# Gelu-branch and first merge projections in turn, attention five steps later, and recurrence weights with hi and lo stacked in the contraction

## The chip, the cores and the metric

The kernel runs on one core of one Trainium2 chip. Its engines are TensorE (PE in the profile, PEld for its weight loads), VectorE (DVE), ScalarE (ACT), GpSimd (POOL) and SyncE (SP), which issues the DMAs. The metric is the device time in microseconds of one execution; the number shown is the median of the runs.

## What is computed

A decoder trunk of two layers on 256 tokens of 1024 features, all in float32: a half-step SwiGLU, a hybrid mixing block, another half-step SwiGLU, and a gated per-layer embedding, each with RMSNorm in front. The change lies in the mixing block alone:

```python
proj = h @ w_in[i]
rx, rgate, q, k, v, f_logit, ga, gb = jnp.split(proj, split_idx, axis=-1)
rx = causal_dwconv(rx, conv_w[i], conv_b[i])
ya = rg_lru(rx, rg_wa[i], rg_ba[i], rg_wx[i], rg_bx[i], rg_lambda[i])
ya = (ya * jax.nn.gelu(rgate)) @ w_rnn_out[i]
yb = forgetting_attention(q, k, v, f_logit, f_b[i], q_norm[i], k_norm[i]) @ w_attn_out[i]
merged = jax.nn.sigmoid(ga + mb_a) * ya + jax.nn.sigmoid(gb + mb_b) * yb
x = x + merged @ w_o[i]
```

`rg_lru` multiplies each of 16 blocks of 64 channels by its own two 64 x 64 matrices (`rg_wa` for the gate r, `rg_wx` for the gate i), takes sigmoids, forms a decay and an input from them, and runs a linear recurrence along the tokens. Attention has 8 heads of 128.

## The kernel before

Activations lie transposed, features on the 128 partitions (8 tiles of 128 features) and 256 tokens along the free dimension. A product in float32 is made from halves: each operand is split into `hi`, its value rounded to the matmul's format, and `lo`, the rest, and hi·hi + hi·lo + lo·hi is accumulated in PSUM (`mm3`, lines 304 to 306 for weights as the stationary operand, 309 to 311 for activations; `mm2`, lines 344 to 347, does two of the three with one matmul of 512 columns).

Weights stream from HBM. The list `plan` gives their order; class `Weights` loads a chunk of about 1 MB into one of three raw buffers `wr` (line 84, on SP's queue), and splits each half of it, a *unit* of eight 128 x 128 tiles, into `wh` on ACT (line 95) and `wl` on DVE (line 96). Five units fit; `W.next()` hands out one and emits the split of the one four units ahead.

The mixing block of a layer goes through these steps in program order:

- Eight `rx` projections. `rx_post` applies the norm, runs the convolution (`conv`) and splits its output `xc` into `xch` (ACT, line 522) and `xcl` (DVE, line 523).
- The `v` projection and a first part of q and k. Between their parts `gates(m)` does the block products of tile m: for each of the two gates a 128 x 128 weight tile with the two 64 x 64 blocks on its diagonal, zeros elsewhere, and `mm3`, so six matmuls of 256 columns. ACT takes the tanh of each gate (`thr`, `thi`, lines 554 and 555), then come two deferred steps, `s1` (clamp of `thr` on DVE; exp, tanh and square on ACT) and `s2` (`tq` on DVE at line 565, and `xc` times the gate i at line 566). `root` takes a square root of all `tq`.
- The remaining q and k projections, with the recurrence (`scan`, lines 575 and 576) between their parts.
- 24 *fillers*, one unit each: 8 for the gelu branch (`f < KT`), which have four more DVE operations and three more ACT operations than the rest, 8 for merge gate A and 8 for merge gate B, which have one DVE and one ACT operation.
- Attention, in four steps for each head (`step_a` transposes, `step_b` scores and softmax, `step_c` transposes, `step_d` the weighted sum into `ot`). They are hung on the parts of the second q and k group and on the fillers through `slots`: head h begins at slot 4 + (5h+1)//2, where slots 0 to 7 are the parts and 8 to 31 the fillers.
- The merge: `ya` (recurrence branch) and `yb` (attention) products by pairs of output tiles, their gated sum `mg`, and the product with `w_o`.

Small steps are handed to a queue (`defer`) and taken from it by `tick` and `drain`. The order in this text is not the order on the engines: the framework's planner (`schedule_with_timeline_sim=True`) orders each engine's instructions by a simulated timeline, with the order of the text as priority, and only marked instructions keep their place.

Of the kernel before, what the change touches and what calls it, by code (L numbers as in the profile page):

```python
# [10 lines left out]
F32 = mybir.dt.float32  # L11
F32R = mybir.dt.float32r
# [4 lines left out]
P = 128  # L17
# [26 lines left out]
HC = S + 4 * P + 1  # L44
WARM = 9
MF, MA, MB, MO = 6, 8, 2, 6


class Weights:
# [70 lines left out]
def trunk(ctx: ExitStack, tc: tile.TileContext, head, xT, pT, vec, w1i, w1o, wf, wqk, wv, wg, wro, wao, wo, w2i, w2o,  # L120
# [16 lines left out]
    def big(shape, dt, s):  # L137
        return bp.tile(shape, dt, name=nm(s), tag="big")
# [21 lines left out]
    for l in range(DEPTH):  # L160
        plan += [(w1i[l, j], [1024, 1024]) for j in range(2 if l == 0 else 0, FT)]
        plan += [(w1o[l, m, :, h * 1408:(h + 1) * 1408], [768, 640]) for m in range(KT) for h in range(2)]
        plan += [(wf[l, 0, c], [1024, 1024]) for c in range(4)]
        plan += [(wv[l, c], [4 * VC, 4 * VC]) for c in range(4)]
        plan += [(wqk[l, qk, cb, hf], [1024, 1024]) for cb in range(2) for qk in range(2) for hf in range(2)]
        plan += [(wf[l, f, c], [1024, 1024]) for f in (1, 2, 3) for c in range(4)]
        plan += [(wrao, [1024, 1024]) for c in range(4) for wrao in (wro[l, c], wao[l, c])]
        plan += [(wo[l, c], [1024, 1024]) for c in range(4)]
        plan += [(w2i[l, j], [1024, 1024]) for j in range(FT)]
        plan += [(w2o[l, m, :, h * 1408:(h + 1) * 1408], [768, 640]) for m in range(KT) for h in range(2)]  # L170
        plan += [(wpg[l, c], [1024, 1024]) for c in range(4)]
# [331 lines left out]
    def mix(l, n, wgp):  # L503
        a = n.act
        R2 = small(TT)
        xc = big([P, KT, S], F32, "xc")
        xch = big([P, KT, S], F32R, "xch")
        xcl = big([P, KT, S], F32R, "xcl")


        def rx_post(m, ps):
            t = rxp[m % NRX]
            V.tensor_tensor(out=t[:, 3:], in0=ps[:, 0:S], in1=n.RB, op=ALU.mult)
            A.activation(out=xc[:, m], in_=t[:, 0:S], func=AF.Identity, scale=col(l, "convw", m), bias=col(l, "convb", m))

            def conv():
                for k in range(1, 4):
                    V.scalar_tensor_tensor(out=xc[:, m], in0=t[:, k:k + S], scalar=col(l, "convw", 8 * k + m),
                                           in1=xc[:, m], op0=ALU.mult, op1=ALU.add)

            def split():
                A.activation(out=xch[:, m], in_=xc[:, m], func=AF.Copy)
                V.tensor_tensor(out=xcl[:, m], in0=xc[:, m], in1=xch[:, m].bitcast(F32), op=ALU.subtract)
            defer(conv, split)

        two = (mmbank, atbank)
# [20 lines left out]

        def gates(m):
            ps = two[m % 2]("g")
            for g in range(2):  # L550
                c = slice((m * 2 + g) * P, (m * 2 + g + 1) * P)
                mm3(ps[:, g * S:(g + 1) * S], wg_hi[:, c], wg_lo[:, c], xch[:, m], xcl[:, m], True, True)
            thr, thi, th, a2 = work(s="thr"), work(s="thi"), work(s="th"), work(s="a2")
            A.activation(out=thr, in_=ps[:, 0:S], func=AF.Tanh, scale=0.5, bias=hcol(l, "ba", m))
            A.activation(out=thi, in_=ps[:, S:], func=AF.Tanh, scale=0.5, bias=hcol(l, "bx", m))
            sc, nsc = sp[:, l, 0, m:m + 1], sp[:, l, 1, m:m + 1]

            def s1():
                V.tensor_scalar(out=thr, in0=thr, scalar1=-1.0, scalar2=None, op0=ALU.max)
                A.activation(out=at[:, m], in_=thr, func=AF.Exp, scale=nsc, bias=nsc)  # L560
                A.activation(out=th, in_=thr, func=AF.Tanh, scale=sc, bias=sc)
                A.activation(out=a2, in_=at[:, m], func=AF.Square)

            def s2():
                V.scalar_tensor_tensor(out=tq[:, m], in0=a2, scalar=1.0, in1=th, op0=ALU.add, op1=ALU.mult)
                V.scalar_tensor_tensor(out=xc[:, m], in0=thi, scalar=1.0, in1=xc[:, m], op0=ALU.add, op1=ALU.mult)
            defer(s1, s2)
# [177 lines left out]
        slots = [[] for _ in range(4 * KT)]  # L745
        for h in range(NH):
            for i, f in enumerate((step_a, step_b, step_c, step_d)):
                slots[4 + (5 * h + 1) // 2 + i].append((f, h))

        def attend(i):  # L750
            for f, h in reversed(slots[i]):
# [34 lines left out]
        qk_group(1, 0, during1(0))  # L786
        qk_group(1, 1, during1(1))
        drain()
        for f in range(3 * KT):
            filler(f)  # L790
            attend(KT + f)
            tick()
        drain()

# [156 lines left out]
def _layout(inputs):  # L951
# [20 lines left out]
                   axis=1)  # L972
    vf = np.concatenate([v, f], axis=2)
    wv = vf.reshape(L, KT, P, 4, VC).transpose(0, 3, 2, 1, 4).reshape(L, 4, P, KT * VC)
    wg = np.zeros((L, P, KT, 2, P), np.float32)
    for i, t in enumerate((g["rg_wa"], g["rg_wx"])):
        t = t.reshape(L, KT, 2, 64, 64)
        for b in range(2):
            wg[:, b * 64:(b + 1) * 64, :, i, b * 64:(b + 1) * 64] = t[:, :, b].transpose(0, 2, 1, 3)
    wg = wg.reshape(L, P, KT * 2 * P)  # L980
    wpe = g["ple_w_proj"].reshape(L, 2, P, KT, P).transpose(0, 2, 3, 1, 4).reshape(L, P, KT * 2 * P)

# [15 lines left out]
    vec[:, :, VEC["fb"]:VEC["fb"] + NH] = g["f_b"][None]  # L998
    put("mba", g["merge_b"][:, :D])
    put("mbb", g["merge_b"][:, D:])  # L1000
    put("ba", g["rg_ba"])
    put("bx", g["rg_bx"])
    put("pb", g["ple_b_gate"])

    w1i = ffn_in(g["ffn1_w_in"])
# [29 lines left out]
```

## Time and profile before

| | |
|---|---|
| median of three runs | 1323.04 us (1323.02 to 1323.09) |
| profiled execution | 1323.63 us, span 1321.8 us |
| PE busy | 1311.8 us (99%), 8610 matmuls |
| DVE busy | 1076.1 us (81%) |
| ACT busy | 815.5 us (62%) |
| DMA | 240.21 MB, mean 182 GB/s |

The span runs from the first to the last instruction; the profiled execution's own time is 1.8 us more. Busy times of one engine count overlapping instructions once; PE's matmuls overlap, so that the duration of one is more than its share of the engine's time.

### The profile page before, as it was taken

How to read it: one execution, taken by the hardware profiler on the slowest of the kernel's cores; microseconds unless marked ns; L12 is line 12 of the kernel's file. 1: busy time of each engine (PE TensorE's matmuls, PEld its weight loads, DVE VectorE, ACT ScalarE, POOL GpSimd, SP SyncE). 2: the span in 40 equal slices, each digit the busy share in tenths (PEclk: the TensorE clock that was granted, in tenths of full speed). 3: DMA queues.
4: the chain of work that ended last, by engine and by line, in shares of the span. 5: the costliest groups of instructions: out<-in, count | busy, mean ns of one | idle time of the engine just before them, and what ended most of it. 6: DMA issues, size and time to landing. Idle time of an engine off the chain costs nothing.

```text
span 1321.8 us, 22442 instructions
## 1 busy us (share of the span) xinstructions
PE 1311.8 (99%) x8610; PEld 1197.7 (91%) x8610; DVE 1076.1 (81%) x2142; ACT 815.5 (62%) x1470; POOL 34.1 (3%) x43
## 2 busy tenths in 40 slices
PE   9999999999999999999999999999999999999997
PEld 8888899889999888889988888998999998888897
DVE  7998769899757899876789877698997678988756
ACT  6665656868655666565566555578677556655653
POOL 1000000020000000000000000000200000000000
PEclk9999999999999999999999999999999999999998
DMA  8654665445435555456545546644543455554650
GB/s 292 243 179 160 212 225 193 158 164 175 151 128 191 196 189 189 162 184 231 187 165 192 188 153 212 241 161 159 193 166 128 161 190 191 192 191 142 213 187 33
DMA packets 37259, 240.21 MB, mean 182 GB/s; under 512 B 4128, under 2 KB 4768, under 8 KB 14368
## 3 DMA queue, kind: packets, MB, share of 16 engines
q1 hardware_dynamic: 36720, 238.25, 51.3%
q8 instruction: 68, 1.11, 0.3%
q10 hardware_dynamic: 432, 0.52, 0.1%
q14 instruction: 39, 0.32, 0.1%
HBM read 237.71 MB, written 1.05 MB: 181 GB/s over the span
## 4 chain that ended last, share of the span: by engine, by line
PE 99%; DMA 0%; DVE 0%; ACT 0%; SPq 0%; POOLq 0%; issue 0%; DVEq 0%
PE mm L347 20%; PE mm L345 11%; PE at L347 11%; PE at L345 6%; PE f L304 3%; PE f L305 3%; PE f L306 3%; PE qk L309 2%; PE qk L311 2%; PE qk L310 2%; PE mm L306 2%; PE mm L304 2%; PE mm L305 2%; PE ya L347 2%; PE mm L344 2%; PE at L344 2%
## 5 line engine op out<-in xcount | busy, mean ns | idle before, releaser
L95 ACT ACTIVATE wh<-wr 128x1024 fp32r<-128x1024 f32 (+2 forms) x476 | 467.4, 986 | 308.0 <-PE mm L347 90.8
L96 DVE TENSOR_TENSOR wl<-wr,wh 128x1024 fp32r<-128x1024 f32 (+2 forms) x476 | 537.7, 1132 | 142.3 <-ACT wh L95 136.9
L347 PE MATMUL mm<-h,wh 128*128 128x512 f32 x616 | 219.2, 394 | 0.0
L347 PE MATMUL at<-h,wh 128*128 128x512 f32 x616 | 218.4, 394 | 0.0
L345 PE MATMUL mm<-h,wl 128*128 128x256 f32 x704 | 182.4, 281 | 0.0
L345 PE MATMUL at<-h,wl 128*128 128x256 f32 x704 | 181.7, 281 | 0.3 <-DVE wl L96 0.2
L347 PE MATMUL mm<-f,wh 128*128 128x512 f32 x504 | 176.8, 394 | 0.0
L345 PE MATMUL mm<-f,wl 128*128 128x256 f32 x528 | 144.0, 280 | 0.0
L345 PEld LDWEIGHTS at<-h,wl 128*128 128x128 f32 x704 | 131.8, 188 | 8.8 <-DVE wl L96 0.8
L345 PEld LDWEIGHTS mm<-h,wl 128*128 128x128 f32 x704 | 131.8, 188 | 7.8 <-DVE wl L96 0.4
L347 PEld LDWEIGHTS mm<-h,wh 128*128 128x128 f32 x616 | 115.6, 188 | 22.5
L347 PEld LDWEIGHTS at<-h,wh 128*128 128x128 f32 x616 | 114.9, 188 | 21.9
L347 PEld LDWEIGHTS mm<-f,wh 128*128 128x128 f32 x504 | 94.4, 188 | 20.8
L304 PE MATMUL f<-h,wh 128*128 128x256 f32 x384 | 108.6, 283 | 0.0
L306 PE MATMUL f<-h,wl 128*128 128x256 f32 x384 | 108.4, 282 | 0.0
L305 PE MATMUL f<-h,wh 128*128 128x256 f32 x384 | 108.4, 282 | 0.0
L345 PEld LDWEIGHTS mm<-f,wl 128*128 128x128 f32 x528 | 99.4, 188 | 2.1
L305 PEld LDWEIGHTS f<-h,wh 128*128 128x128 f32 x384 | 72.3, 188 | 0.1
L304 PEld LDWEIGHTS f<-h,wh 128*128 128x128 f32 x384 | 72.3, 188 | 0.1
L306 PEld LDWEIGHTS f<-h,wl 128*128 128x128 f32 x384 | 72.4, 189 | 0.0
L381 ACT ACTIVATE sum<-mm 128x256 f32<-128x256 f32 x112 | 40.2, 376 | 49.3 <-PE mm L347 49.3
L382 DVE TENSOR_TENSOR sum<-mm,sum 128x256 f32<-128x256 f32 x112 | 44.9, 417 | 15.0 <-ACT sum L381 15.0
(291 smaller groups left out, 2857.6 us busy)
## 6 DMA issues: line engine op xcount, KB each, us to landing
wr<-in_w2i SPq DMA_DIRECT2D x44, 1024.0 KB, 4.8
wr<-in_w1i SPq DMA_DIRECT2D x41, 1024.0 KB, 4.8
wr<-in_wf SPq DMA_DIRECT2D x32, 1024.0 KB, 4.8
wr<-in_w1o SPq DMA_DIRECT2D x32, 704.0 KB, 4.0
wr<-in_w2o SPq DMA_DIRECT2D x32, 704.0 KB, 4.0
wr<-in_wqk SPq DMA_DIRECT2D x16, 1024.0 KB, 4.8
wr<-in_wv SPq DMA_DIRECT2D x8, 1032.0 KB, 4.9
wr<-in_wro SPq DMA_DIRECT2D x8, 1024.0 KB, 4.8
```

The lines of the kernel that those rows point to most:

```text
L95: self.nc.scalar.activation(out=hi[:, c], in_=src[:, c], func=AF.Copy)
L96: self.nc.vector.tensor_tensor(out=lo[:, c], in0=src[:, c], in1=hi[:, c].bitcast(F32), op=ALU.subtract)
L304: T.matmul(ps, lhsT=wh, rhs=xh, start=first, stop=False)
L305: T.matmul(ps, lhsT=wh, rhs=xl, start=False, stop=False)
L306: T.matmul(ps, lhsT=wl, rhs=xh, start=False, stop=last)
L309: T.matmul(ps, lhsT=xh, rhs=wh, start=first, stop=False)
L310: T.matmul(ps, lhsT=xh, rhs=wl, start=False, stop=False)
L344: T.matmul(ps, lhsT=wh, rhs=t, start=True, stop=False, skip_group_check=True)
L345: T.matmul(ps[:, 0:S], lhsT=wl, rhs=t[:, 0:S], start=False, stop=False, skip_group_check=True)
L347: T.matmul(ps, lhsT=wh, rhs=t, start=False, stop=last, skip_group_check=True)
L381: A.activation(out=o, in_=ps[:, S:], func=AF.Copy)
L382: V.tensor_tensor(out=o, in0=ps[:, 0:S], in1=o, op=ALU.add)
```

## The change

Three edits, all in the mixing block.

1. *Stacked weights.* For each tile of 128 channels, which holds two blocks b of 64, the rows of the new 128 x 128 weight tile b hold block b's matrix twice, once in the lower and once in the upper 64 rows, and its columns hold both gates, r and i (in the other order for b = 1). The moving operand `xs[b]` stacks hi and lo of block b's 64 channels on the partitions. One matmul with the hi weights and one with the lo weights then give both gates of the block, with one product more than `mm3` has (lo·lo). Four matmuls of 256 columns take the place of six. The split writes `xs` by halves of the partitions, two ACT and two DVE instructions in place of one and one; half of them write to the other half of the partitions than they read. ACT's two tanh now give r and i of one block each (`t2`, a tile of 512 columns from the pool with three buffers), a DMA on SP's queue moves the half that holds i to the partitions of its channels in `thi` (two DMAs of 64 partitions x 1 KB per tile), and the clamp writes `thr` by two instructions of 64 partitions. The biases are put in the same order on the host.
2. *Order of the fillers.* Instead of 8 gelu, 8 gate A, 8 gate B: two gelu and two gate A in turn, four times, then 8 gate B. The chunks of `wf` are loaded in the same order.
3. *Attention five slots later.* Head h begins at slot 9 + (5h+1)//2 (`AT0`).

```diff
+AT0 = 9
 ...
-        plan += [(wf[l, f, c], [1024, 1024]) for f in (1, 2, 3) for c in range(4)]
+        plan += [(wf[l, f, c], [1024, 1024]) for c in range(4) for f in (1, 2)]
+        plan += [(wf[l, 3, c], [1024, 1024]) for c in range(4)]
 ...
-        xch = big([P, KT, S], F32R, "xch")
-        xcl = big([P, KT, S], F32R, "xcl")
+        xs = [big([P, KT, S], F32R, "xs") for _ in range(2)]
+        lower, upper = slice(0, 64), slice(64, P)
 ...
             def split():
-                A.activation(out=xch[:, m], in_=xc[:, m], func=AF.Copy)
-                V.tensor_tensor(out=xcl[:, m], in0=xc[:, m], in1=xch[:, m].bitcast(F32), op=ALU.subtract)
+                for b, own, other in ((0, lower, upper), (1, upper, lower)):
+                    A.activation(out=xs[b][own, m], in_=xc[own, m], func=AF.Copy)
+                    V.tensor_tensor(out=xs[b][other, m], in0=xc[own, m], in1=xs[b][own, m].bitcast(F32),
+                                    op=ALU.subtract)
 ...
         def gates(m):
             ps = two[m % 2]("g")
-            for g in range(2):
-                c = slice((m * 2 + g) * P, (m * 2 + g + 1) * P)
-                mm3(ps[:, g * S:(g + 1) * S], wg_hi[:, c], wg_lo[:, c], xch[:, m], xcl[:, m], True, True)
+            for b in range(2):
+                c = slice((m * 2 + b) * P, (m * 2 + b + 1) * P)
+                T.matmul(ps[:, b * S:(b + 1) * S], lhsT=wg_hi[:, c], rhs=xs[b][:, m], start=True, stop=False)
+                T.matmul(ps[:, b * S:(b + 1) * S], lhsT=wg_lo[:, c], rhs=xs[b][:, m], start=False, stop=True)
             thr, thi, th, a2 = work(s="thr"), work(s="thi"), work(s="th"), work(s="a2")
-            A.activation(out=thr, in_=ps[:, 0:S], func=AF.Tanh, scale=0.5, bias=hcol(l, "ba", m))
-            A.activation(out=thi, in_=ps[:, S:], func=AF.Tanh, scale=0.5, bias=hcol(l, "bx", m))
+            t2 = work2(s="tg")
+            for b, own, other in ((0, lower, upper), (1, upper, lower)):
+                c = slice(b * S, (b + 1) * S)
+                A.activation(out=t2[:, c], in_=ps[:, c], func=AF.Tanh, scale=0.5, bias=hcol(l, ("ba", "bx")[b], m))
+                nc.sync.dma_start(out=thi[own], in_=t2[other, c])
 ...
             def s1():
-                V.tensor_scalar(out=thr, in0=thr, scalar1=-1.0, scalar2=None, op0=ALU.max)
+                for b, own in ((0, lower), (1, upper)):
+                    V.tensor_scalar(out=thr[own], in0=t2[own, b * S:(b + 1) * S], scalar1=-1.0, scalar2=None,
+                                    op0=ALU.max)
 ...
-                slots[4 + (5 * h + 1) // 2 + i].append((f, h))
+                slots[AT0 + (5 * h + 1) // 2 + i].append((f, h))
 ...
-        for f in range(3 * KT):
+        turns = [f + m for m in range(0, KT, 2) for f in (0, 1, KT, KT + 1)] + list(range(2 * KT, 3 * KT))
+        for i, f in enumerate(turns):
             filler(f)
-            attend(KT + f)
+            attend(KT + i)
             tick()
```

On the host, `_layout` builds the new weight tiles and puts the two biases in the order of the gates' halves.

## Rows read from the trace of the kernel before

**Rows 1.** The page's head: the span, the busy time of each engine (share of the span, number of instructions), and the granted TensorE clock in 40 equal slices of the span, in tenths.

```profile
span 1321.8 us, 22442 instructions
PE 1311.8 (99%) x8610; PEld 1197.7 (91%) x8610; DVE 1076.1 (81%) x2142; ACT 815.5 (62%) x1470; POOL 34.1 (3%) x43
...
PEclk9999999999999999999999999999999999999998
```

**Rows 2.** The waits of TensorE over the whole span, the first and the last of the five that are listed, longest first: who waited for whom, us in total, times, longest.

```profile
PE warm L871 <- POOL ones L189: 1.1, 1, 1.1
...
PE at L344 <- ACT wh L95: 0.2, 1, 0.2
```

**Rows 3.** The instructions that touch the gates' PSUM tile `g`, one of the three kinds of matmul: shortest, median and longest duration in ns, first and last start in us.

```profile
L305 PE MATMUL g<-xcl,wbh x32: 277/280/288, 226.9 to 903.8; 128*128 128x256 f32 x32
```

**Rows 4.** TensorE in order of time, the gates of the first two channel tiles in layer 0: the first two of the twelve matmuls, and the projection's matmul behind the twelfth. Columns: start us, duration us, engine, line, operation, out<-in, shape of the weights, of the moving operand.

```profile
226.81 0.28 PE L304 MATMUL g<-xch,wbh 128*128 128x256 f32 x1
226.93 0.28 PE L305 MATMUL g<-xcl,wbh 128*128 128x256 f32 x1
...
228.22 0.28 PE L309 MATMUL v<-wh,h 128*128 128x258 f32 x1
```

**Rows 5.** ScalarE and then VectorE in order of time around the same gates and the next pair (columns as in rows 4, with idle time before and what ended it in brackets).

```profile
228.65 0.46 ACT L554 ACTIVATE thr<-g,half 128x256 f32<-128x256 f32 x1
229.00 0.47 ACT L555 ACTIVATE thi<-g,half 128x256 f32<-128x256 f32 x1
...
230.55 0.42 DVE L566 SCALAR_TENSOR_TENSOR xc<-thi,xc 128x256 f32<-128x256 f32 x1
...
235.02 0.42 DVE L565 SCALAR_TENSOR_TENSOR tq<-a,th 128x256 f32<-128x256 f32 x1 [0.21 <-ACT a L562]
...
238.84 0.29 DVE L559 TENSOR_SCALAR thr<-thr 128x256 f32<-128x256 f32 x1
239.05 0.42 DVE L566 SCALAR_TENSOR_TENSOR xc<-thi,xc 128x256 f32<-128x256 f32 x1
239.38 0.41 DVE L523 TENSOR_TENSOR xcl<-xc,xch 128x256 fp32r<-128x256 f32 x1
```

**Rows 6.** Busy time by stretch of layer 0: the window and its length; busy us and number of instructions of PE, PEld, DVE, ACT, POOL; granted clock; DMA share; GB/s.

```profile
215.00:255.00 40.00, 40.00 (x292) 37.92 (x291) 36.24 (x86) 33.86 (x67) 0.00 (x0) 1.00 0.46 159
255.00:289.00 34.00, 34.00 (x153) 27.57 (x152) 29.80 (x58) 22.94 (x30) 9.28 (x7) 1.00 0.43 155
289.00:311.00 22.00, 22.00 (x188) 21.91 (x187) 21.99 (x49) 15.95 (x34) 1.98 (x2) 1.00 0.62 210
311.00:333.00 22.00, 22.00 (x189) 22.00 (x188) 20.30 (x51) 16.00 (x35) 0.00 (x0) 1.00 0.51 186
333.00:353.00 20.00, 20.00 (x174) 20.00 (x173) 14.55 (x33) 13.73 (x32) 0.00 (x0) 1.00 0.39 144
```

**Rows 7.** Waits over the whole span, of all engines and then of SP's queue: who waited for whom, us in total, times, longest.

```profile
ACT wh L95 <- DMA wr<-in_w1i: 3.2, 4, 1.8
...
DVE tq L575 <- ACT tq L570: 4.2, 2, 2.1
...
SPq L84 <- DVE wl L96: 387.5, 87, 13.7
```

**Rows 8.** DMAs: the issue of the 256 KB load of `p` on SP (ns: shortest, median, longest) and its us from issue to landing; then two lines of the table of issues (count, KB each, median us to landing).

```profile
L440 SPq DMA_DIRECT2D p<-in_pT x2: 425/426/426, 290.1 to 941.9; - x2
...
DMA to landing us min/median/max: 5.0/5.3/5.5
...
wr<-in_wqk SPq DMA_DIRECT2D x16, 1024.0 KB, 4.8
...
out_dram<-out SPq DMA_DIRECT2D x2, 128.0 KB, 2.1
```

**Rows 9.** TensorE in order of time, the first matmul of the first filler and the first of the second filler that reads low halves (the 27th `f` matmul); then, of VectorE, the operation that writes those low halves.

```profile
289.35 0.28 PE L304 MATMUL f<-h,wh 128*128 128x256 f32 x1
...
292.51 0.28 PE L306 MATMUL f<-h,wl 128*128 128x256 f32 x1
...
288.49 1.22 DVE L96 TENSOR_TENSOR wl<-wr,wh 128x1024 fp32r<-128x1024 f32 x1
```

**Rows 10.** TensorE in order of time, attention and the second merge product of layer 0: the last score matmul of heads 0, 3 and 7; the second matmul of head 7's weighted sum and the `yb` behind its last; the first matmuls of `yb` that read head 7 (x2), of `ya` 4 and of `ya` 5. The VectorE row writes the low half of head 7's `ot`.

```profile
293.43 0.28 PE L711 MATMUL s<-dk,aq 128*128 128x256 f32 x1
...
338.59 0.28 PE L711 MATMUL s<-dk,aq 128*128 128x256 f32 x1
...
377.21 0.28 PE L711 MATMUL s<-dk,aq 128*128 128x256 f32 x1
...
390.16 0.28 PE L739 MATMUL o<-pl,vh 128*128 128x256 f32 x1
...
390.68 0.45 PE L347 MATMUL yb<-ot,wh 128*128 128x512 f32 x1
...
391.30 0.42 DVE L335 TENSOR_TENSOR ot<-o,ot 128x256 fp32r<-128x256 f32 x1 [2.35 <-ACT ot L334]
...
393.81 0.40 PE L345 MATMUL yb<-ot,wl 128*128 128x256 f32 x2
...
398.44 0.39 PE L344 MATMUL ya<-yr,wh 128*128 128x512 f32 x1
...
401.22 0.39 PE L344 MATMUL ya<-yr,wh 128*128 128x512 f32 x1
```

More of the change, by code (lines that the diff above doesn't have):

```diff
@@ L974, in _layout @@
     wv = vf.reshape(L, KT, P, 4, VC).transpose(0, 3, 2, 1, 4).reshape(L, 4, P, KT * VC)
-    wg = np.zeros((L, P, KT, 2, P), np.float32)
+    wg = np.zeros((L, 2, 64, KT, 2, 2, 64), np.float32)
     for i, t in enumerate((g["rg_wa"], g["rg_wx"])):
@@ L978, in _layout @@
         for b in range(2):
-            wg[:, b * 64:(b + 1) * 64, :, i, b * 64:(b + 1) * 64] = t[:, :, b].transpose(0, 2, 1, 3)
+            wg[:, :, :, :, b, i ^ b] = t[:, :, b].transpose(0, 2, 1, 3)[:, None]
     wg = wg.reshape(L, P, KT * 2 * P)
@@ L1000, in _layout @@
     put("mbb", g["merge_b"][:, D:])
-    put("ba", g["rg_ba"])
-    put("bx", g["rg_bx"])
+    rb, ib = (g[n].reshape(L, KT, 2, 64) for n in ("rg_ba", "rg_bx"))
+    put("ba", np.concatenate([rb[:, :, 0], ib[:, :, 0]], axis=2))
+    put("bx", np.concatenate([ib[:, :, 1], rb[:, :, 1]], axis=2))
     put("pb", g["ple_b_gate"])
```

## The prediction, made before the change was run

> **What bounds the kernel now.** Read the busy table and the 40 slices first [rows 1]: TensorE (PE) is busy 99% of the span at a granted clock of 0.9 or more, the upper of its levels (2.4 GHz), in every slice but the last, VectorE (DVE) 81%, ScalarE (ACT) 62%. The profiled execution took 1323.63 us for a span of 1321.8; the median of the runs is 1323.04, that is 0.59 less, and this 0.59 is carried over at the end. A busy share of 99% can still hide waiting, so the waits of PE come next [rows 2]: five of 0.2 to 1.1 us, 2.8 in all, and the longest is that of the warm-up before the first weights. PE therefore owes nothing to any other engine between its first weights and its last tile. The kernel lasts as long as PE's queue of matmuls, and only two things can move the end: fewer or cheaper matmuls, or a new wait of PE.
>
> Then the price of a matmul. The groups say 280 ns for one of the gates' matmuls [rows 3], but these durations overlap: in the timeline of one pair of gates twelve start between 226.81 and 228.22 us [rows 4], one each 1.41/12 = 0.1175 us, the neighbouring starts 0.11 to 0.13 apart. What a removed matmul gives back is the distance of starts, not the duration. Taken by duration the change would seem to be worth 32 x 0.28 = 9.0 us; the rows exclude that.
>
> **The change part by part.** *Stacked block weights.* Per tile of 128 channels the gates need six matmuls of 256 columns now and four after: two fewer, for 8 tiles and 2 layers 32 fewer. 32 x 0.1175 = 3.76 us; with the bounds of the starts 32 x 0.11 = 3.5 to 32 x 0.13 = 4.2. Weight loads are one for each matmul at 0.12 us distance and go with it. The contraction is over 128 partitions before and after, so I price the new matmul like the old one.
>
> The Trainium skill, "TensorE: Matmul & The Clock Gate", section "Back-to-back issue gap", gives the isolated distance as columns divided by 2.4 plus 2.5 ns, which is 109 ns here against the 117.5 measured. By it the sum would be 32 x 0.109 = 3.5 us.
>
> *The split of the convolution's output.* One ACT and one DVE instruction per tile become two of each, on half the partitions. No row shows an instruction on 64 partitions. Bounds: half the time each (nothing added) or the full time each. By starts, a DVE operation of 256 columns takes 0.33 us (239.05 to 239.38), the clamp of `thr` 0.21 (238.84 to 239.05), an ACT operation 0.35 (228.65 to 229.00) [rows 5]. The clamp also becomes two. So DVE gets 0 to 8 x (0.33 + 0.21) = 4.3 us more per layer and ACT 0 to 8 x 0.35 = 2.8. I take the full 4.3 and 2.8. Between 215 and 289 us, where this work lies, DVE idles 3.76 + 4.20 = 8.0 us, and ACT 6.1 us in the first of the two stretches alone [rows 6]. About 2.1 of DVE's is the wait for the square root (4.2 us in two layers) [rows 7] and is not to be had, so 5.9 us hide 4.3: cost nothing. If that cover were gone, DVE would be late with the low halves of the weights, `wl`, which is the rival below.
>
> *The shuffle of `thi`.* Two DMAs per tile, 16 per layer, on SP's queue, each waiting for a tanh. Behind a waiting one stand the weight loads. An issue takes SP 0.43 us, going by the 256 KB load of `p` [rows 8]: 6.8 us per layer, while SP spends 387.5 us of the run waiting only for `wl` to free a raw buffer [rows 7]. Of ACT's waits for landing weights the longest group is 3.2 us in all, for `w1i` [rows 7]; none is in this stage. I take nothing for SP. The landing lies between 2.1 us (128 KB of output) and 5.3 (256 KB of `p`, more than the 4.8 of a whole 1024 KB weight load) [rows 8]. Its reader, the DVE product L566, now starts 1.1 us after its tanh ends (229.47 to 230.55), but `tq` of these gates runs only at 235.02 [rows 5]: standing behind that, 5.5 us after the tanh, it finds the data landed. I take nothing.
>
> *The order of the fillers, and attention five steps later.* No matmul is added, so on PE both are worth nothing by themselves: it does not wait there now. They move DVE's load. Each gelu filler has four more DVE operations than a merge filler, and today the eight gelu fillers come together: DVE is busy 22.0 of 22.0 and 20.3 of 22.0 us from 289 to 333 (0.96), then 14.6 of 20 (0.73) [rows 6]. In turn, the same work is spread at about the mean, 0.84 of the time. Each set of weights is only loaded in another order, with the same count. Cost and gain: nothing, as long as attention ends in time (second rival).
>
> **Sum.** 1323.63 - 3.76 = 1319.87 in a profiled execution, less 0.59: 1319.3 us. A change of 0.2% (2.6 us) is about what a measurement of this kernel can tell from none, and this one is 0.28%.
>
> **Rivals.**
> *A. The forecast: no new wait.* 1319.3, from 3.5 to 4.2 us saved, with up to 1 us either way for a new interleaving: 1318 to 1320.2.
>
> *B. VectorE is short at the first fillers.* The tightest place I find: the first filler's 24 matmuls start at 289.35, the second's first one that reads `wl` is at 292.51, and that `wl` is ready at 288.49 + 1.22 = 289.71: 2.8 us of slack [rows 9]. DVE runs without a pause there. If none of the 4.3 us is absorbed earlier, PE waits 4.3 - 2.8 = 1.5 us per layer, 3.0 in all: 1322.3, no change that can be told. If PE's 1.9 us per layer also arrive there against a DVE that keeps its hour, it is 3.4 per layer: 1326.1. For it: DVE's 22 of 22. Against it: its idle time just before, the ACT copy of these weights that waits for PE to free a buffer and so moves with PE, and attention's first operations, which leave this place.
>
> *C. Attention ends too late, and the second merge product waits (slower).* Every `yb` needs all eight heads of `ot`. Heads now end their scores at 293.43 (first), 338.59 (fourth) and 377.21 (eighth); the last weighted sum is at 390.16, 12.95 later, its `ot` is written by 391.72 and first read at 393.81 [rows 10]. Five steps are five times 24 matmuls, 5 x 2.85 = 14.3 us; less the 1.9 saved before, the first head moves to 305.8. PE's other work after 390.68 is the 7.76 us of `yb` up to 398.44, less the ten matmuls in it that read the last head (four at 2.78/16 us and six at 0.1175: 1.4 us), and one more `ya` (2.78, 398.44 to 401.22), for which a buffer of split weights is free: it lasts until 399.8 now, 397.9 after, so the last weighted sum must start by 396.4 (1.5 before its `ot`). Hence the point that decides: (396.4 - 12.95 - 305.8)/7 = 11.1 us per head. Today's pace is 15.1 us over the first three heads, where DVE is full, 9.7 over the last four, 12.0 over all. At 12.0 the sum starts at 402.8: 6.4 us of waiting per layer, 12.8 in all, 1332.1. I expect about 10.5, because DVE's load is then 0.84 throughout, between the two: 392.3, with 4 us to spare.
>
> *D. The shuffles land behind weight loads.* If L566 keeps its place, DVE stands 2.1 - 1.1 to 5.3 - 1.1, that is 1.0 to 4.2 us, in each of six sets of gates: 6 to 25 us per layer. With the 4.3, less 5.9 of idle time and 2.8 of slack, PE would lose 1.6 to 20.6 us per layer, in the middle 11: 1341. For it: `p`, a quarter of a weight load, took longer than one. Against it: the 5.5 us above.
>
> The Trainium skill, "DMA: Bandwidth & Descriptors", section "Queues, rings and completion order", says that a DMA engine consumes one queue's descriptors in ring order; by that rule a shuffle behind a weight load on the same queue waits for it. The 5.3 us of `p` agree; no row here has a transfer of 64 partitions.
>
> **Chances and range.** A 0.60; B 0.20, because the slack is thin but the cover larger than the addition; C 0.11; D 0.07; 0.02 for a better interleaving than today's. Faster: A and the last, 0.62. Within 0.2%: 0.17 of B, 0.02 of C, 0.03 of D, 0.22. Slower: 0.03 of B, 0.09 of C, 0.04 of D, 0.16. The range runs from 1317.8 (4.2 us and 1 us of interleaving) to 1324.0 (B's 1322.3 and half the way to its worse end); C's and D's slow part and B's tail stay out, 0.16 to 0.18. The likeliest case alone: 1318.0 to 1320.2.
>
> **What would show it.** Right: 64 gate matmuls where there are 96, starts 0.117 us apart; PE's list of waits still under 3 us; the first filler about 1.9 us earlier in layer one (287.4); DVE and ACT busier before 289 and DVE less full from 289 to 333. B would be a PE wait for `wl` near 290, C a PE wait for `ot` (or for `wh` behind it) near 398, D a DVE wait for a DMA in front of L566's successor. Wrong above all if the gates' four matmuls stand farther apart than 0.12 us, or if PE shows a wait of more than 1 us per layer in the fillers or at the merge.

## The result and the profile after

The changed kernel is slower: 1333.84 us (1333.73 to 1334.74, five runs) against 1323.04 (1322.97 to 1323.09, five runs), a ratio of 1.0083 [1.0072, 1.0095]. The profiled execution took 1333.74 us for a span of 1331.5. Its head, beside [rows 1]:

```profile
span 1331.5 us, 22496 instructions
...
PE 1311.8 (99%) x8578; PEld 1196.9 (90%) x8578; DVE 1090.9 (82%) x2174; ACT 822.9 (62%) x1486; POOL 32.5 (2%) x43
...
PEclk9999999999999999999999999999899999999999
```

There are 32 matmuls fewer, 14.8 us more of VectorE, and one slice with a granted clock under 0.9. The waits of TensorE, beside [rows 2] (the other entries are those of before, 0.3 to 1.1 us):

```profile
PE f L306 <- DVE qk L675: 6.2, 2, 3.1
PE s L306 <- ACT aq L711: 3.7, 2, 1.8
```

Once a layer the first filler `f` waits 3.1 us for VectorE's `qk`, and just before it the first head's scores `s` wait 1.8 us for ScalarE's `aq`, the split operands of the scores. In time, layer 0 before the change:

```profile
251.09 0.28 DVE L559 TENSOR_SCALAR thr<-thr 128x256 f32<-128x256 f32 x1
254.10 0.28 DVE L559 TENSOR_SCALAR thr<-thr 128x256 f32<-128x256 f32 x1
...
266.46 2.00 ACT L570 ACTIVATE tq<-tq,tiny 128x2048 f32<-128x2048 f32 x1
...
286.41 0.68 DVE L663 TENSOR_TENSOR qk<-qk,s 128x512 f32<-128x512 f32 x1
```

and after:

```profile
268.31 0.58 DVE L570 TENSOR_SCALAR thr<-tg 64x256 f32<-64x256 f32 x2
271.50 0.58 DVE L570 TENSOR_SCALAR thr<-tg 64x256 f32<-64x256 f32 x2
...
276.61 2.00 ACT L582 ACTIVATE tq<-tq,tiny 128x2048 f32<-128x2048 f32 x1
...
278.64 1.77 DVE L587 TENSOR_TENSOR tq<-tq,xc 128x256 f32<-128x256 f32 x5 [2.04 <-ACT tq L582]
...
289.54 0.68 DVE L588 TENSOR_TENSOR_SCAN xc<-a,tq 128x256 f32<-128x256 f32 x1
...
292.11 0.68 DVE L675 TENSOR_TENSOR qk<-qk,s 128x512 f32<-128x512 f32 x1
...
292.85 0.58 PE L306 MATMUL f<-h,wh 128*128 128x256 f32 x1 [3.11 <-DVE qk L675]
```

This is a chain. The last two tiles' clamps of `thr` run 17 us later than before; the one square root over all tiles follows 10.1 us later; the scans stand behind it; and the product that normalises the first bank of the second q and k group, 5.7 us later, ends at 292.79. That product is the last reader of a PSUM bank. In `qk_group(1, ...)` both token halves take their banks from `mmbank`, one of the two pools of PSUM banks, where the fillers take theirs too, so the first filler cannot begin before it. Before, the product ended at 287.09 and the filler came at 289.35 [rows 9]: 2.3 us of slack, now a wait.

Behind the wait TensorE is slow for a while. Busy time by windows (columns as in [rows 6]), the wait, what follows it, and the same place in layer 1:

```profile
290.00:293.00 3.00, 0.15 (x1) 0.15 (x1) 3.00 (x7) 0.00 (x0) 0.72 (x1) 0.91 0.75 281
...
292.80:295.80 3.00, 2.95 (x14) 2.95 (x15) 3.00 (x7) 0.00 (x0) 0.70 (x2) 0.50 0.85 299
...
295.80:300.00 4.20, 4.20 (x37) 4.20 (x37) 4.00 (x13) 1.61 (x3) 1.81 (x2) 0.99 0.12 47
...
949.00:952.00 3.00, 2.82 (x13) 2.82 (x14) 3.00 (x8) 0.00 (x0) 0.70 (x2) 0.50 0.88 282
...
952.00:955.50 3.50, 3.50 (x22) 3.50 (x22) 2.34 (x6) 1.01 (x2) 1.94 (x2) 0.63 0.19 75
```

TensorE was busy 0.15 of 3 us, and the granted clock then stands at 0.50, the lower level (1.2 GHz): 14 matmuls in 2.95 us, 0.21 each against 0.1175 [rows 4], 1.3 us lost. In layer 1 it is 13 in 2.82 and 22 in 3.50, some 2.2 us lost. The account of the profiled executions: -3.7 for the matmuls (below), +6.2 and +3.7 of waits, +3.5 of clock, together +9.7; measured 1333.74 - 1323.63 = +10.1.

The saving itself is there. TensorE, the gates of the first two tiles, beside [rows 4]:

```profile
226.74 0.28 PE L557 MATMUL g<-xs,wbh 128*128 128x256 f32 x1
226.85 0.28 PE L558 MATMUL g<-xs,wbl 128*128 128x256 f32 x1
...
227.69 0.28 PE L311 MATMUL v<-wh,h 128*128 128x258 f32 x1
```

Eight starts take 0.95 us where twelve took 1.41: 0.46 for two tiles, 3.7 for 16.

### The profile page after: what moved, and what is told of

Read it like the earlier page. It is cut to its first block, busy times and chain, and to the rows that moved or that the text cites. A ratio compares the mean times of both kernels' runs of the same rounds, so it can differ in the third digit from the quotient of the medians.

```text
span 1331.5 us, 22496 instructions
## 1 busy us (share of the span) xinstructions
PE 1311.8 (99%) x8578; PEld 1196.9 (90%) x8578; DVE 1090.9 (82%) x2174; ACT 822.9 (62%) x1486; POOL 32.5 (2%) x43
## 4 chain that ended last, share of the span: by engine, by line
PE 94%; DVE 4%; ACT 1%; DMA 1%; issue 0%; SPq 0%; POOLq 0%; DVEq 0%
PE mm L349 19%; PE mm L347 11%; PE at L349 11%; PE at L347 6%; PE f L306 4%; PE f L307 4%; PE f L308 4%; PE mm L306 2%; PE mm L308 2%; PE mm L307 2%; PE ya L349 2%; PE mm L346 2%; PE at L346 2%; PE o L349 1%; PE pl L306 1%; PE pl L308 1%
## 5 line engine op out<-in xcount | busy, mean ns | idle before, releaser
L306 PE MATMUL f<-h,wh 128*128 128x256 f32 x384 | 111.0, 289 | 6.2 <-DVE qk L675 6.2
L307 PE MATMUL f<-h,wh 128*128 128x256 f32 x384 | 110.1, 287 | 0.0
L306 PEld LDWEIGHTS f<-h,wh 128*128 128x128 f32 x384 | 74.1, 193 | 6.5 <-DVE qk L675 6.5
L307 PEld LDWEIGHTS f<-h,wh 128*128 128x128 f32 x384 | 74.2, 193 | 0.0
```

Of the source, the lines that this page charges most:

```text
L306: T.matmul(ps, lhsT=wh, rhs=xh, start=first, stop=False)
L307: T.matmul(ps, lhsT=wh, rhs=xl, start=False, stop=False)
```

## The experiments

Ratios are against the kernel before, measured beside each run (its medians lie between 1323.00 and 1323.51), with 95% intervals; "early" and "late" say where the forget gate's chain (log-sigmoid, running sum, `dc` and `dk`, which attention needs) stands in the queue of small steps (defined at e9).

| run | VectorE's split and clamp | chain | time, us | ratio |
|---|---|---|---|---|
| before / e13 | one each | early / late | 1323.04 / 1323.03 | 1 / 0.9999 [0.9990, 1.0009] |
| after / e9 | two halves each | early / late | 1333.84 / 1332.63 | 1.0083 / 1.0069 [1.0054, 1.0084] |
| e5 / e10 | one each, no stacking | early / late | 1329.37 / 1318.67 | 1.0044 [1.0029, 1.0059] / 0.9966 [0.9953, 0.9979] |
| e7 / e11 | one half, the other on GpSimd | early / late | 1326.80 / 1324.30 | 1.0029 [1.0017, 1.0041] / 1.0006 [0.9997, 1.0015] |
| e17 / e14 | both halves on GpSimd | early / late | 1324.51 / 1320.28 | 1.0008 [0.9999, 1.0017] / 0.9979 [0.9970, 0.9989] |

**Which edit.** e1 makes the stacked weights alone (fillers and `AT0` as before), e2 the two edits of order alone.

> The stacked weights with their split and shuffles alone; the fillers in the old order, attention at its old slots. Three theories of the 10.8 us lost. Shuffle: the DMAs of thi land behind weight loads, the last gates' products, the square root and the recurrence's scans come 10 us later on VectorE and push the norms of q and k, whose PSUM banks the first filler needs; it lies in this edit, so 1330 to 1336 here, with PE waits near 290 us and 945 us. Work: VectorE's added instructions alone do the same; also 1330 to 1336. Order: the two edits of the order do it; then 1319 to 1320 here and no PE wait over 1 us.

> The kernel before with the two edits of the order alone (gelu and gate A fillers in turn, attention five slots later), block products unstacked. Shuffle and work: nothing to wait for, 1322.5 to 1323.5, as before. Order: 3.8 us worse than the changed kernel, 1336 to 1338, with the same waits of PE at the first filler.

e1: 1335.52 us, 1.0092 [1.0077, 1.0107], with the same waits (`f` for `qk` 7.6, `s` for `aq` 3.2). e2: 1323.26, 0.9997 [0.9987, 1.0007], no new wait over 0.5 us. The loss is the stacked edit's.

**The shuffles.** After's rows for `thi`: the issue on SP (ns: shortest, median, longest), and us from issue to landing.

```profile
L565 SPq DMA_DIRECT2D thi<-tg x32: 461/544/1221, 228.7 to 912.4; - x32
...
DMA to landing us min/median/max: 1.9/5.1/7.4
```

They land late, but VectorE's list of waits has one wait for them, 1.3 us in the whole run. e3 lets ACT write both halves of the gate itself, e6 leaves the transfers out and lets the product read `t2` in place (so the values of the gate i are those of other channels or of r).

```diff
-A.activation(out=t2[:, c], in_=ps[:, c], func=AF.Tanh, ...)         # e3 alone
-nc.sync.dma_start(out=thi[own], in_=t2[other, c])                   # e3 and e6
+A.activation(out=t2[own, c], in_=ps[own, c], func=AF.Tanh, ...)      # e3
+A.activation(out=thi[own], in_=ps[other, c], func=AF.Tanh, ...)      # e3
+V.scalar_tensor_tensor(out=xc[:, m], in0=t2[:, S:], ...)             # e6, in s2
```

> The changed kernel without the DMAs: ScalarE writes the gate i of each block to its own channels itself, by tanh from the other half of the PSUM partitions, so four tanh on 64 partitions in place of two on 128 (some 5.6 us more ScalarE per layer) and the same VectorE instructions as the changed kernel. Shuffle: the square root comes back from 276.6 us to 265 to 268, PE's waits at the first filler fall from 9.9 us in all to under 3, 1319 to 1323. Work or order: the waits stay, 1331 to 1335.

> The changed kernel without the 32 DMAs: the product at the gate i reads the tanh where it lies, so half the channels get the wrong gate (this part, the shuffle, is left out), and one work tile per gate less is held; everything else as in the changed kernel. Shuffle: the square root comes back to 266 to 268 us and PE no longer waits, 1319 to 1321. Work: no more than some of the 1.3 us DVE wait per layer is won, norms of the second group still 4 to 6 us late, 1329 to 1334.

e3: 1340.95 us, 1.0132 [1.0117, 1.0147]; e6: 1341.85, 1.0138 [1.0123, 1.0154]. Both are slower than after, and in both TensorE waits 12.5 to 12.9 us for `aq` of the first head, whose scores the planner now puts ahead of the fillers. e3 also loads ACT (its four tanh of 64 partitions take 464 to 469 ns each, as long as those of 128). Taking the transfers away gives nothing back, but in these two runs the order changed with them, and the square root came still later (279.5 and 282.5 us). That the transfers are not the cause rests on e10 and e14 below, which keep them and lose nothing; why the planner's order gets worse without them isn't settled.

**The PSUM banks.** e4: the first two fillers take `atbank` in place of `mmbank`.

> The changed kernel with one edit: the first two fillers of a layer accumulate in the other four PSUM banks, which q's and k's second group doesn't hold. Shuffle and work: the square root stays late (about 276 us), but the first filler no longer waits for the norms of q and k; PE's 9.9 us of waits at the first filler and the drop of its clock behind them go, 1319 to 1323. If the banks are not the last link (attention's place in the order, or the low halves of the weights are), the waits stay and it takes 1330 to 1335.

```profile
PE o L346 <- DVE sum L384: 2.6, 2, 1.3
PE f L306 <- DVE qk L675: 1.8, 2, 0.9
PE ya L346 <- ACT wh L96: 1.8, 2, 0.9
PE ya L347 <- DVE wl L97: 1.5, 2, 0.8
```

1330.80 us, 1.0056 [1.0041, 1.0071]. The waits of TensorE in e4 show what follows: the one for `qk` falls from 6.2 to 1.8, and 5.9 us turn up at the merge (`ya`, and `o`, the product with `w_o`), where VectorE and ACT are now late. The bank is the last link; the lateness behind it is VectorE's.

**VectorE's added work.** The groups by shape from 204 to 275 us (us in all, mean ns), after and then e5, which makes the split and the clamp as one instruction of 128 partitions each (and so leaves the stacking out: `xs[0]` is all hi, `xs[1]` all lo, and the gates' values are not the reference's; transfers, matmuls and order stay):

```profile
L527 DVE TENSOR_TENSOR xs<-xc,xs 64x256 fp32r<-64x256 f32 x16 | 6.7, 420 | 0.5
...
L570 DVE TENSOR_SCALAR thr<-tg 64x256 f32<-64x256 f32 x16 | 4.5, 282 | 0.2
```

```diff
+A.activation(out=xs[0][:, m], in_=xc[:, m], func=AF.Copy)
+V.tensor_tensor(out=xs[1][:, m], in0=xc[:, m], in1=xs[0][:, m].bitcast(F32), op=ALU.subtract)
...
+V.tensor_scalar(out=thr, in0=t2[:, 0:S], scalar1=-1.0, scalar2=None, op0=ALU.max)
```

> The changed kernel with VectorE's and ScalarE's split and clamp as before, one instruction each on 128 partitions per tile, with the four matmuls, the shuffles and the order of the changed kernel; it leaves out the stacking of hi and lo and the choice of each half's gate, so the gates are of other products. Work (VectorE's 64-partition instructions, which take 6.9 us more per layer up to the norms of q's and k's second group, set the loss): no wait of PE at the first filler, the four norms 286 to 288 us, and the saving of the 32 matmuls shows: 1319 to 1320. Shuffle: the square root stays at 276 us or so and PE still waits, 1331 to 1335.

Its waits of TensorE, the clamp of tile 6, and ACT in order of time:

```profile
PE f L306 <- DVE qk L671: 6.3, 2, 3.2
```

```profile
265.55 0.28 DVE L567 TENSOR_SCALAR thr<-tg 128x256 f32<-128x256 f32 x1
```

```profile
256.51 0.60 ACT L663 ACTIVATE qsq<-qk 128x512 f32<-128x512 f32 x1 [1.06 <-DVE s L665]
...
273.90 2.01 ACT L578 ACTIVATE tq<-tq,tiny 128x2048 f32<-128x2048 f32 x1
```

1329.37 us (1328.01 to 1331.82; the trace is of the slowest): 4.5 of the 10.8 us come back, not all. VectorE's split and clamp are as light as before, and still the square root is at 273.9: the clamps of tiles 6 and 7 run at 265.6 and 268.9. So work is not the whole cause. (The row of `qsq` shows a smaller effect: `t2` of those two tiles holds two of the three buffers it shares with the squares for the norms, and the second square waits for the first to be read.) e7 keeps the stacking and puts the half of b = 1 on GpSimd, `(V, G)[b]` in place of `V` at both places; e8 does the same with edits 2 and 3 undone.

> The changed kernel with the second block's half of the split and of the clamp on GpSimd, which is 3% busy; the same result. VectorE is left with 16 instructions of 64 partitions per layer in place of 32. Work: VectorE has only 1 to 1.5 us more per layer than before, the norms come back to 286 to 289 us, 1319 to 1323, if GpSimd's operations take under 2 us. Shuffle: 1331 to 1335.

> The same with fillers and attention in the order before: stacked weights and half the small work on GpSimd alone. Work: as the kernel before it, within 2 us, 1319 to 1324; if attention's place matters once VectorE is relieved, this is 2 to 6 us slower than the one with the new order. Shuffle: 1333 to 1336.

e7: 1326.80 (ten runs, 1324.35 to 1331.64); e8: 1329.24, 1.0039 [1.0024, 1.0054]. e7 is slower than expected, e8 2.4 us slower again. Less on VectorE is faster, with a wait of 2.8 us per layer left at the first filler.

**The place of the last clamps.** Small steps are taken from one queue. The forget gate's chain is put on it at the first part of q and k, ahead of `s1` and `s2` of tiles 6 and 7, and puts itself in front again after each step. e9 puts it there two parts later:

```diff
-                if w == 0 and u == 0:
+                if w == 0 and u == 2:
                     defer_gen(forget())
```

> The changed kernel, except that the forget gate's chain (log-sigmoid of z, its running sum, dc and dk) is put on the queue of small steps after the last tile's gates, not after gates(5); so s1 and s2 of tiles 6 and 7 stand ahead of it in the text. Nothing is left out. Theory Place (part of the loss is that the clamps of tiles 6 and 7 are now taken behind that chain, at 268.3 and 271.5 us where they ran at 251.1 and 254.1 before, which moves the square root by 10 us and the scans and q/k norms behind it): the square root comes back to 267 to 270 us, the norm of the second group's first bank to 289 or earlier, the wait of TensorE at the first filler falls from 3.1 us to under 1.5 per layer, and the time to 1325 to 1329. Theory Work (VectorE's total before that norm alone decides, its order does not): norm at 291 to 293, waits as they were, 1332 to 1335.

> The kernel with one split and one clamp of 128 partitions per tile (which leaves out the stacking of hi and lo and takes the gates from the wrong places for half of the channels), with the forget gate's chain on the queue after the last tile's gates. Together with the single instructions this takes away both suspected causes, VectorE's extra work and the late clamps. Theory Place: what the single instructions alone left (1329.4, with a wait of 3.2 us per layer at the first filler, square root at 273.9) goes too: square root by 268, no wait over 1 us at the first filler, 1319 to 1321. Theory Work: no gain over 1329. Theory Transfers (the shuffles on SP's queue hold something else up): 1324 to 1329 with a wait left in the gates or for weights.

> The changed kernel with the b = 1 half of split and clamp on GpSimd (1326.8 by itself, wait of 2.8 us per layer at the first filler, square root at 272.9) and with the forget gate's chain on the queue after the last tile's gates. Nothing is left out. Theory Place: square root by 269, norm of the second group's first bank by 287, wait at the first filler under 1 us per layer, 1319.5 to 1322, faster than the kernel before. Theory Work: 1326 to 1327, no different from the half on GpSimd alone.

> The changed kernel with the forget gate's chain on the queue after the last tile's gates, and the first two fillers in the attention's PSUM banks, so that they need not wait for the q/k norms. All work of the change stays on VectorE. Banks alone gave 1330.8. Theory Place with its banks: 1322 to 1326, no wait at the first filler, small waits later at the merge. Theory Work (whatever is relieved, VectorE's 6.9 us more per layer come back as a wait somewhere before the merge's end): 1329 to 1332.

e9: 1332.63 us. The square root is back at 267.6, and the time is not. TensorE in e9:

```profile
PE qk L311 <- DVE qk L675: 7.0, 2, 3.5
PE qk L312 <- DVE wl L97: 1.6, 2, 0.8
```

Now the norms of the first group are late, with the forget chain among them, and the second group waits for their bank at 285.8: the same VectorE, one place earlier. e12 (e9 with e4's banks): 1333.38, 1.0078 [1.0062, 1.0095], slower than either theory had it, with the same 7.0 us; the banks of e4 are no longer the ones that matter. e10, both causes away, in the longest of its waits of TensorE and ACT in time:

```profile
PE warm L881 <- POOL ones L191: 1.1, 1, 1.1
```

```profile
262.18 2.01 ACT L578 ACTIVATE tq<-tq,tiny 128x2048 f32<-128x2048 f32 x1 [0.18 <-DVE tq L573]
```

1318.67 us, no wait of TensorE over 1.1, the first filler at 286.89. With transfers, four matmuls and both edits of order in it, it comes out where the forecast was. e11: 1324.30, in between and slower than expected.

**A version that is faster, and what carries it.** e13 is the kernel before with the late chain; e14 to e16 are after with the late chain and `G` in place of `V` for split and clamp (e14), the clamp (e15), the split (e16).

> The kernel before with only the forget gate's chain on the queue after the last tile's gates. It tells whether that move has a gain of its own. Theory Place (the move only makes room where VectorE is late, and the kernel before has no wait of TensorE to lose): 1322.7 to 1323.8, within 0.05% of before. Rival (the move is a gain by itself, and the 1318.7 of the single instructions is half due to it): 1320 to 1321.5.

> The changed kernel with the late forget chain and all low-half splits and clamps on GpSimd, so that VectorE has 2.76 + 1.62 = 4.4 us less per layer than in the kernel before; nothing is left out. GpSimd takes 0.7 to 1.9 us for each, some 32 us per layer in the 50 us of the gates. Theory Work + Place: no wait at the norms, 1318.5 to 1320.5, if GpSimd's slower splits do not reach TensorE; if they do, waits at the gates and 1321 to 1326. Rival (the stacked operands or the shuffles cost time by themselves): over 1323 with the waits still at the q/k norms.

> The changed kernel with the late forget chain and only the clamps (both halves) on GpSimd; the splits, 6.7 us per layer where the single ones took 2.8, stay on VectorE, so VectorE has 4.0 - 1.6 = 2.3 us more per layer than before. Nothing is left out. Theory Work + Place: a wait of at most 0.7 us per layer at the q/k norms, 1319.5 to 1322.

> The changed kernel with the late forget chain and only the low-half splits (both halves) on GpSimd; the clamps, 4.5 us per layer where they took 1.6, stay on VectorE, so VectorE has 2.9 - 2.8 = 0.1 us more per layer than before. Nothing is left out. Theory Work + Place: as the kernel before in the norms, no wait there, 1318.8 to 1320.5, unless the splits on GpSimd (0.7 to 1.9 us each, two after each other) come too late for the gates, which would show as waits of TensorE for xs.

e13: nothing gained, so the late chain is no gain by itself. e14 computes everything and beats both kernels, 1320.28 us, 0.9979 [0.9970, 0.9989]; its head, its waits, its first filler, and two groups from 204 to 262 us:

```profile
PE 1307.7 (99%) x8578; PEld 1192.4 (90%) x8578; DVE 1079.2 (82%) x2110; ACT 821.7 (62%) x1486; POOL 102.2 (8%) x107
```

```profile
PE s L306 <- ACT aq L711: 0.6, 1, 0.6
PE qk L311 <- DVE qk L675: 0.5, 1, 0.5
```

```profile
287.43 0.28 PE L306 MATMUL f<-h,wh 128*128 128x256 f32 x1
```

```profile
L527 POOL TENSOR_TENSOR xs<-xc,xs 64x256 fp32r<-64x256 f32 x16 | 17.2, 1074 | 18.4 <-issue 12.2 <-ACT xs L526 5.5
L521 DVE SCALAR_TENSOR_TENSOR xc<-rxp,vt,xc 128x256 f32<-128x256 f32 x24 | 13.8, 607 | 0.1
```

GpSimd has what VectorE lost, and the convolution's steps (`xc`) on VectorE, 478 ns in the same group of the kernel before, take 607 beside it:

```profile
L518 DVE SCALAR_TENSOR_TENSOR xc<-rxp,vt,xc 128x256 f32<-128x256 f32 x24 | 10.8, 478 | 0.0
```

So VectorE is not less busy than in the kernel before: 76.4 of the 85 us from 204 to 289, against 76.1, and 79.5 in after.

e15: 1324.01, 1.0005 [0.9995, 1.0014]; e16: 1327.35, 1.0031 [1.0019, 1.0043], both slower than expected, with waits of 3.0 and 4.1 us for `wl` in the q and k projections. Either half of the added work left on VectorE costs the gain. In e16 it is not that half alone: its expectation counted 0.1 us more on VectorE than in the kernel before, but beside GpSimd's splits the convolution's steps took 590 ns (478 in the kernel before) and the clamps 385 (282 in after), and VectorE was busy 43.9 of the 46 us from 204 to 250, against 41.2 in e14 and 44.2 in after. With the clamps alone on GpSimd (e15) the convolution's steps took 492. Last, e17 is e14 with the chain early, e18 is e14 without edits 2 and 3.

> The kernel of e14 (all low-half splits and clamps on GpSimd, 1320.3 us) with the forget gate's chain back where the changed kernel has it. Nothing is left out. Theory Place (the chain ahead of the last two tiles' clamps moves the square root by some 10 us whoever does the clamps, and the q/k norms with it): square root at 272 or later, a wait of 1 to 3 us per layer at the first filler, 1323 to 1328. Theory Work (with VectorE relieved the place does not matter): 1320 to 1321.

> The kernel of e14 without edits 2 and 3: fillers and their weights in the order of the kernel before, attention begun at slot 4. Nothing is left out. Theory Neutral (edits 2 and 3 are worth nothing, as when they were made alone): 1319.5 to 1321.5. Rival (with less slack at the norms it helps that attention's first steps are not at the first fillers): a wait of 1 us or more per layer there or for wl, 1322 to 1325.

e17: 1324.51, square root at 270.0, and these waits:

```profile
PE f L306 <- DVE qk L675: 2.5, 1, 2.5
PE f L306 <- ACT wh L96: 2.1, 1, 2.1
```

The first is in layer 1; in layer 0 the first filler waits for `wh`, not for the norm. The place is worth 4.2 us even with VectorE relieved. e18: 1323.93, 1.0006 [0.9997, 1.0016], slower than e14 by 3.6 us. The rival's time came, its sign did not: it wanted 1 us or more per layer at attention's first steps or for `wl`. The waits of TensorE in e18 that e14 lacks:

```profile
PE ya L345 <- ACT wh L96: 1.7, 2, 0.9
...
PE s L306 <- DVE aq L712: 0.8, 2, 0.4
```

At the first steps it is 0.4 us per layer (`s`), and more at the merge (`ya`). They do not add up to 3.6; the rest is not accounted for.

## Why the prediction was wrong

*What bounds the kernel, and the price of a matmul*: right. Waits, clock and saving account for after within 0.4 us (in e4, e16 and e18 the time is 1 to 3 us longer than the listed waits and the saving give, not explained), and the 3.76 us (3.7 measured) are there when no wait eats them: e14's first filler is at 287.43, where 287.4 was forecast, and e10's time is 1318.67 against 1319.3. That e10 gains 4.4 us by these medians (4.8 against the kernel before beside it, 1323.51) instead of 3.7 is about the one us allowed for interleaving and isn't explained further.

*The split and the clamp*: the first step that failed. The full price of a half was taken as 0.33 and 0.21 us, the distance of starts of neighbours on 128 partitions [rows 5], and the added 4.3 us per layer as an upper bound. VectorE in after:

```profile
231.75 0.87 DVE L527 TENSOR_TENSOR xs<-xc,xs 64x256 fp32r<-64x256 f32 x2
232.65 0.59 DVE L570 TENSOR_SCALAR thr<-tg 64x256 f32<-64x256 f32 x2
233.27 0.42 DVE L527 TENSOR_TENSOR xs<-xc,xs 64x256 fp32r<-64x256 f32 x1
```

and wholes in e10, from 204 to 275 us (us in all, mean ns):

```profile
L526 DVE TENSOR_TENSOR xs<-xc,xs 128x256 fp32r<-128x256 f32 x8 | 3.3, 418 | 0.0
...
L567 DVE TENSOR_SCALAR thr<-tg 128x256 f32<-128x256 f32 x8 | 2.3, 286 | 0.0
```

A half takes as long as a whole, 420 and 282 ns against 418 and 286, and two halves do not overlap: 0.87 and 0.59 us for two, and the next instruction starts 0.03 later still. So a tile pays 0.90 - 0.33 and 0.62 - 0.21 us more, 7.8 per layer. By busy time alone, without those pauses, the 32 halves take 6.7 + 4.5 = 11.2 us where the 16 wholes held VectorE for 4.4 (start to next start): 6.8, the 6.9 of the expectations.

The Trainium skill, "VectorE: DVE Perf Modes", section "Two Vector instructions with no wait between them", says that an instruction whose input or output begins in another group of 32 partitions than the last one's is held until all earlier ones have finished. Halves that alternate between lower and upper partitions are such a case, and the 0.87 and 0.59 us agree. So does e9, where other work came between the halves of one clamp:

```profile
259.59 0.28 DVE L570 TENSOR_SCALAR thr<-tg 64x256 f32<-64x256 f32 x1
259.79 0.41 DVE L578 SCALAR_TENSOR_TENSOR xc<-thi,xc 128x256 f32<-128x256 f32 x1
260.21 0.29 DVE L570 TENSOR_SCALAR thr<-tg 64x256 f32<-64x256 f32 x1
```

By the order of the text the first is the lower half (the trace doesn't tell the halves apart), and begins at the same partition as the instruction behind it, which starts 0.20 us later, as behind a whole; the upper half starts only when that one has ended. Half the partitions alone, then, does not cost the overlap; the alternation does. That page bore on the change and was not drawn on.

*The cover*: the second. Of VectorE's 8.0 us of idle time 5.9 were taken as room for any work before 289. But the work behind the square root cannot move ahead of it, and the root needs all eight tiles. I priced the clamps as if each kept its hour; the last two went from 251.1 and 254.1 to 268.3 and 271.5, behind the forget chain. e10 against e5 (10.7 us for the chain's place alone) and e9 against after (1.2) show that the two causes do not add: take one away and the other still makes a bank late. Why the planner took those clamps ahead of the chain before and no longer does isn't settled; what differs is that `thr` is now first written by the clamp.

*The slack*: the third. Rival B was right that VectorE is short at the first fillers, but I measured its slack at `wl` (2.8 us) and not at the norm that frees the fillers' bank (2.3 us). Had I, 4.3 us, with none of it absorbed earlier, would already have given a wait of 2 us per layer; with 7.8 and the place of the clamps it was 3.1 and 1.8. (Half the way from 1322.3 to B's 1326.1 is 1324.2, not the 1324.0 of the range; it changes nothing.)

*After a wait*: the fourth. B's price was the wait alone. The clock adds 3.5 us, a third of the loss.

What was to show the forecast wrong, a wait of over 1 us per layer in the fillers, is what after's list begins with.

*Rival C* fell: no list has a wait for `ot`, with attention five steps later in e2, e10 and e14. Its point of decision was closer than the forecast had it: in e10 a head took (376.5 - 300.5)/7 = 10.9 us, where 11.1 was the limit and 10.5 expected, and what saved it is that the first head's scores ended at 300.5, not at 305.8; that C fell is in part luck. The 0.84 behind the 10.5 is also low: by the lengths of the three stretches of [rows 6] VectorE was busy 0.89 of the time. *Rival D* fell too: the transfers took up to 7.4 us, more than its 5.3, and cost VectorE 1.3 us in all.

*Edits 2 and 3 at nothing*: right by themselves (e2), wrong beside the first edit, where they are worth 3.6 us (e18 against e14, both with GpSimd and the late chain; e1 against after and e8 against e7 point the same way, with 1.7 and 2.4, but their intervals overlap). That it is attention's place that is worth it, and not the order of the fillers, is not shown: the two edits were never parted, and e18's added waits lie more at the merge than at the first fillers.

Open: the 1.6 us between e14 and e10. e14 has 1.1 us of waits in the mixing block that e10 lacks, but e10 has 0.9 more elsewhere, for `wh` and `wl`.

## What to carry to other kernels

When matmuls are saved by rearranging an operand, price the rearrangement on the engine that does it, with its true shape: half the partitions was no cheaper here, and alternating halves cost more than two wholes. When a busy engine gets more work, ask of its next releases (PSUM banks first) which has the least slack, and of each step that waits for all tiles what delays the last one. And a wait of the engine that bounds the kernel is not its whole price: here 4.9 us of it per layer cost another 1.3 to 2.2 in the clock (in e7 a wait of 2.8 cost nothing in one layer and about 1 us in the other).

## What the runs showed of the hardware

- VectorE: 64 x 256 elements took 420 (subtract) and 282 ns (clamp), 128 x 256 took 418 and 286 in e10; alternating halves did not overlap, one half in e9 did overlap the whole instruction behind it (0.20 us from start to start). ACT: a tanh of 64 partitions 464 to 469 ns, of 128 partitions 464.
- TensorE's granted clock fell to 0.50 after a wait of 3.1 us that followed one of 1.8, and the next 13 matmuls of 256 columns stood 0.21 us apart. In e7, after one wait of 2.8 us, it stayed at 1.00 in layer 0 and stood at 0.51 from 944 to 947 us in layer 1.
- GpSimd took 1074 ns for 64 x 256 in e14, and slowed VectorE: the convolution's steps went from 478 to 607 ns. The Trainium skill, "SBUF — State Buffer", section "Who interferes with whom", says that a VectorE instruction with two inputs in SBUF and a GpSimd one that reads SBUF share a read port, one after the other; the two numbers agree. The clamp, with one input, went from 282 in after to 385 ns in e16, where GpSimd does the splits; why isn't shown.
- 64 KB transfers from SBUF to SBUF landed 1.9 to 7.4 us after issue: 1.9 and 2.1 the two issued at 228.7 us with no weight load just ahead, up to 7.4 those issued at 254.0, right behind a weight load on the same queue.
